# The high part of each weight tile by a casting DMA in the place of a rounding on GpSimd

## The chip, the cores and the metric

The kernel runs on one core of one Trainium2 chip. The metric is the time of one execution in device microseconds (us), as the median of several runs. The engines of a core work side by side, each on its own queue of instructions in a fixed order: TensorE (PE in the profile; PEld is its weight load), VectorE (DVE), ScalarE (ACT), GpSimd (POOL) and SyncE (SP). An instruction waits at the head of its queue until what it needs is there, and all behind it waits with it. DMAs are issued by instructions that stand in such a queue too.

## The reference

The reference is one decoder block for 1024 tokens of 1024 channels: eight heads of forgetting attention and eight of stick-breaking attention, cross-attention to 256 memory tokens, and a gated feed-forward net with a short causal convolution. Cut to its skeleton:

```
h = rmsnorm(x, attn_norm_g)
proj = h @ w_in                       # fq, fk, fv, sq, sk, sv, f_logit
fox_o = forgetting_attention(fq, fk, fv, cumsum(log_sigmoid(f_logit + b_forget)))
sb_o = stick_breaking_attention(sq, sk, sv)
x = x + concat(rmsnorm(fox_o), rmsnorm(sb_o)) @ w_out
x = x + memory_cross_attention(rmsnorm(x), rmsnorm(mem), w_mq, w_mkv, w_mo)
u = causal_dwconv(rmsnorm(x, ffn_norm_g) @ w_up, conv_w, conv_b)
gate, val = split(u)
x = x + (silu(gate) * val) @ w_down
out = rmsnorm(x, final_norm_g)
```

All inputs and the output are float32.

## The kernel before

Matrix products take their operands in the type fp32r, which holds fewer bits than float32. To keep the accuracy, each operand is split into a high part (the value rounded to fp32r) and a low part (the value less its high part), and each product is three matmuls: high by high, high by low, low by high (`mm3`, L100 to L104).

The weights lie in DRAM as pieces of 128 partitions by 1024 columns of float32, 512 KB each, in the order of use (`w[i]`). In the first half of the program a piece is fetched by `getw(i)`, the function that `make_w` returns (L88 to L98). It takes two tiles of 128x1024, `whi` and `wlo`, from a pool with two buffers of each, and works in two halves of 512 columns: SP issues the DMA of the raw half into a tile `wraw` (L94, a pool of three), POOL rounds it into `whi` (L95), DVE subtracts to get `wlo` (L96). `getw` is called 68 times: for the values (`load_v`, two pieces per pair of heads, both in use together), the queries and keys (`load_qk`, one piece each), the keys and values of the memory (L434 on, eight and eight pieces), the projection of the mixed heads (`mixed_out`, four calls of two pieces that are in use together to the end of the call), the queries to the memory (`mem_probs`, two times eight pieces) and a part of the output projection of the memory heads (two times two pieces). With two buffers, the tile of piece n is filled again for piece n+2, once the last matmul on piece n is through. The tiles of raw halves have a pool of their own, so a raw half can be in SBUF while its `whi` is still in use. From the rest of the output projection on, weights are loaded in other ways, and `getw` is not called again.

What else stands on POOL in this half: the multiplication of each stick-breaking row by its running product (L334), the division of each forgetting row by its sum (L320), the power -0.5 of the norms (L86), and the division of the memory's probabilities (L550). What else stands on DVE: the low parts of the attention's rows (L363), the running products (L332), maxima and sums.

The order of each engine's instructions is not that of the source. A scheduler places them, with its own estimates of how long each takes; it interleaves matmuls on weights with those of the attention, so a piece can be filled while PE has other work. That order is fixed when the program is built.

Of the kernel before, what the change touches and what calls it, by code (L numbers as in the profile page):

```python
# [29 lines left out]
# pairs of heads: one of each kind shares the projection of the values  # L30
KINDS = ("s", "f")

# columns of the per-channel parameters
# [11 lines left out]
def hybrid_block(ctx, tc, x, mem, w, wf, pcol, bfg, fing, out):  # L45
# [14 lines left out]
    # ---------------- constants  # L60
# [20 lines left out]
    # ---------------- helpers  # L81
    def rsqrt_mean(dst, ss, n, cnt):
        """dst = (ss / cnt + eps) ** -0.5 for n columns"""
        V.tensor_scalar(out=dst[:, :n], in0=ss[:, :n], scalar1=1.0 / cnt, scalar2=EPS,
                        op0=ALU.mult, op1=ALU.add)
        G.tensor_tensor(dst[:, :n], dst[:, :n], mhalf[:, :n], op=ALU.pow)  # L86

    def make_w(rp, wp):  # L88
        def get(i):
            hi = wp.tile([P, 1024], F32R, tag="whi", name=f"whi{i}")  # L90
            lo = wp.tile([P, 1024], F32R, tag="wlo", name=f"wlo{i}")
            for c in (slice(0, 512), slice(512, 1024)):
                raw = rp.tile([P, 512], F32, tag="wraw", name=f"wraw{i}", bufs=3)
                nc.sync.dma_start(raw, w[i, :, c])  # L94
                G.tensor_scalar(out=hi[:, c], in0=raw, scalar1=1.0, scalar2=0.0, op0=ALU.mult, op1=ALU.add)  # L95
                V.tensor_tensor(lo[:, c], raw, hi[:, c].bitcast(F32), op=ALU.subtract)  # L96
            return hi, lo
        return get  # L98

    def mm3(o, lt, rt, start, stop):  # L100
        """o += l^T r for operands in two exact parts"""
        T.matmul(o, lt[0], rt[0], start=start, stop=False)  # L102
        T.matmul(o, lt[0], rt[1], start=False, stop=False)  # L103
        T.matmul(o, lt[1], rt[0], start=False, stop=stop)  # L104

    def split(hi, lo, ps, scale):
        """hi + lo = ps * scale, exactly"""
        if isinstance(scale, float):
            A.activation(hi, ps, AF.Copy, scale=scale)
        else:  # L110
            A.activation(hi, ps, AF.Identity, scale=scale)
        V.scalar_tensor_tensor(out=lo, in0=ps, scalar=scale, in1=hi.bitcast(F32),
                               op0=ALU.mult, op1=ALU.subtract)

    def norm_half(src_tiles, gcol, hi, lo, pst, wk, n=4, tags=(("T", 2),), xtag="xn", eng=V):
        """rmsnorm of n blocks of tokens, transposed into hi/lo [P, KC, n*P]"""
        ss = small.tile([P, 4], F32, tag="ss", name="ss")
        rs = small.tile([P, 4], F32, tag="rs", name="rs")
        xn = []
        for j in range(n):  # L120
            xs = src_tiles[j]
            t = wk.tile([P, D], F32, tag=xtag, name="xn")
            A.activation(t, xs, AF.Square, accum_out=ss[:, j:j + 1])
            rsqrt_mean(rs[:, j:j + 1], ss[:, j:j + 1], 1, D)
            if eng is V:
                V.tensor_scalar(out=t, in0=xs, scalar1=rs[:, j:j + 1], scalar2=None, op0=ALU.mult)
            else:
                G.tensor_scalar(out=t, in0=xs, scalar1=rs[:, j:j + 1], scalar2=0.0, op0=ALU.mult, op1=ALU.add)
            xn.append(t)
        for kc in range(KC):  # L130
            tg, nb = tags[kc % len(tags)]
            pt = pst.tile([P, 512], F32, tag=tg, name="ptn", bufs=nb)
            for j in range(n):
                T.transpose(pt[:, j * P:(j + 1) * P], xn[j][:, kc * P:(kc + 1) * P], ident)
            split(hi[kc], lo[kc], pt[:, :n * P], col(gcol + kc))

    # ================= token mixing =================
# [3 lines left out]
    # four slots of [P, 4096] for the transposed activations; the last pair's queries, keys and  # L141
    # values leave room for eight more tiles of [P, 1024]
# [20 lines left out]
    def eight(nm, n):  # L163
        """eight tiles of [P, 1024] as two lists of n views"""
        t = [qkp["s"].tile([P, 1024], F32R, tag=g, name=f"{nm}_{g}{i}", bufs=b)
             for g, b, i in (("q", 2, 0), ("q", 2, 1), ("k1", 2, 0), ("k1", 2, 1), ("k2", 1, 0))]
        v5 = vp.tile([P, 2, 1024], F32R, tag="v", name=nm + "_v0")
        v7 = vp.tile([P, 2, 1024], F32R, tag="v", name=nm + "_v1")
        t += [v5[:, 0, :], v5[:, 1, :], v7[:, 0, :]]
        w_ = 4096 // n  # L170
        t = [x_[:, c:c + w_] for x_ in t for c in range(0, 1024, w_)]
        return t[:n], t[n:]
# [47 lines left out]
    # forget gates: -cumsum(log sigmoid(f + b)) as [head, token]  # L220
    def forget():
# [12 lines left out]
        # -log sigmoid(z) = max(-z, 0) + ln(1 + exp(-|z|))  # L234
# [4 lines left out]
    def load_v(pr):  # L239
        """values of a pair of heads of each kind, [token, block, head, hi|lo]"""  # L240
# [21 lines left out]
    def load_qk(kind, pr):  # L262
        """two heads: Q = [hi;lo], K1 = [hi;hi] on the contraction rows; K2 = lo of both"""
# [59 lines left out]
    def sb_row(i, sts, p):  # L323
        """sigmoid(z_s) times the product of 1 - sigmoid(z_j) = sigmoid(-z_j) over j > s"""
# [6 lines left out]
        # running product from the right end; no factor is above 1, so the minimum changes nothing  # L331
# [4 lines left out]
    def attend(kind, h, a, vt, hq, qkt, ost):  # L336
        """one head; the output goes to rows a*64.. of the pair's staging tiles"""
# [51 lines left out]
    for pr in range(4):  # L389
        vt = load_v(pr)  # L390
        for ki, kind in enumerate(KINDS):
# [9 lines left out]
            for g in range(2):  # L401
# [10 lines left out]
                # squares, summed over the pairs  # L412
# [10 lines left out]
    # memory keys and values  # L423
# [28 lines left out]
    # ================= projection of the mixed heads =================  # L452
# [59 lines left out]
    # ================= attention to the memory =================  # L512
# [67 lines left out]
    # the output projection of the memory heads has the form of the feed-forward net's (below): a = the  # L580
    # heads' outputs (halves of the tokens x halves of the channels), b = the weights
# [24 lines left out]
    # in the order b11, b12, b22, b21  # L606
# [4 lines left out]
    # t1 and t3 in the places of b11 and b12  # L611
# [11 lines left out]
    def pairs(t):  # L623
        """[hi | lo] of an operand of [P, 512]"""
        return t[:, :512], t[:, 512:]
# [12 lines left out]
    def mo_product(fa, fb, tags, done, deep=False):  # L638
        """fa(f), fb(f): the operands' values for the channels f; done(j, bank) for each 128 tokens"""
# [47 lines left out]
    # ================= feed-forward net =================  # L687
    # up: products of 2 x 2 blocks (gate | value channels, halves of the contraction, halves of the
    # tokens) in Winograd's form of Strassen's scheme, seven products of blocks in the place of eight:
    #   [c11 c12]   [a11 a12] [b11 b12]     s1 = a21 + a22, s2 = s1 - a11, s3 = a21 - a11, s4 = a12 - s2  # L690
    #   [c21 c22] = [a21 a22] [b21 b22]     t1 = b12 - b11, t2 = b22 - t1, t3 = b12 - b22, t4 = b21 - t2
    #   c11 = a11 b11 + a12 b21             u = a11 b11 + s2 t2, v = u + s3 t3
    #   c12 = u + s1 t1 + s4 b22            c21 = v + a22 t4,    c22 = v + s1 t1
# [42 lines left out]
    # operands of the weights  # L736
# [73 lines left out]
    # second half of the tokens  # L810
# [123 lines left out]
    # down: the same scheme with a = the activations (halves of the tokens x halves of the channels)  # L934
    # and b = the weights (halves of the channels x halves of the outputs); a product runs over all of
    # its channels in four banks, one for 128 tokens of each half
# [10 lines left out]
    # first and second half: a11 | a21 and b11 | b12, later a12 in the place of a11, b21 in that of b11  # L947
# [34 lines left out]
    def op_tile(nm):  # L982
        """[hi | lo] of an operand"""
        tag = ("whi" if nm == "a" else "wlo") if step % 2 == 0 else "xn"
        pool = wp if step % 2 == 0 else wk
        return pairs(pool.tile([P, 1024], F32R, tag=tag, name=f"op{nm}"))

    def dn_product(fa, fb, held=0, done=None):
        """fa(f), fb(f): the operands' values for the channels f; the last held of them are used bank
        by bank, done(j, bank) after each"""  # L990
# [25 lines left out]
    # p1 = a11 b11  # L1016
# [3 lines left out]
    # p7 = (a21 - a11) (b12 - b22)  # L1020
# [5 lines left out]
    # p5 = (a21 + a22) (b12 - b11)  # L1026
# [6 lines left out]
    # p6 = s2 t2  # L1033
# [9 lines left out]
    # p3 = s4 b22  # L1043
# [25 lines left out]
    # p4 = a22 t4: the second half of the tokens is done  # L1069
# [5 lines left out]
    # p2 = a12 b21  # L1075
# [7 lines left out]
def arrange(inputs):  # L1083
    """Lays the inputs out in the order in which the kernel reads them."""
    import numpy as np

    def lhs(m):  # [K, 128] -> [128, K/128, 128]
        return m.reshape(-1, P, m.shape[1]).transpose(1, 0, 2).reshape(P, -1)

    def blocks(m, k, c):  # [K, c] in pieces of k row blocks -> [n, 128, k*c]  # L1090
        return [lhs(m[i * k * P:(i + 1) * k * P]) for i in range(m.shape[0] // (k * P))]
# [60 lines left out]
```

## Time and profile before

| | us |
|---|---|
| median of 3 runs | 1697.02 |
| lowest and highest run | 1696.34 and 1701.86 |
| span of the profiled execution | 1694.0 |

The page gives no other time of the profiled execution than its span; the median of the runs lies 3.0 us above it. The page and the answers of the trace name instructions by line, engine, operation, and out<-in by the names in the program; "x136" counts them. Behind a group's busy time and the mean duration of one stands the idle time of the engine just before them, with what ended it. In a timeline, each row has its start, its length, and in brackets the idle time ahead of it.

### The profile page before, as it was taken

Reading aid. Unit: us, or ns where it says so; the run is one execution under the profiler, and the core shown is the slowest. Engines: PE = TensorE matmul, PEld = TensorE weight load, DVE = VectorE, ACT = ScalarE, POOL = GpSimd, SP = SyncE. Lnnn points to the kernel's source line nnn. Section 1 sums busy time; section 2 is a strip of 40 time slices with the busy share of each in tenths; the row PEclk is TensorE's granted clock in tenths of the full one; section 3 lists DMA queues with packets and bytes.
Section 4 is the critical chain, followed back from the end, with each engine's and each line's share of the span. In section 5 each row is a group of like instructions: output and inputs, shape, how many; then the busy total and the mean of one; then the engine's idle time right before and its main releaser. Section 6 shows DMA issues by size and latency. Waiting matters only on the chain.

```text
span 1694.0 us, 21858 instructions
## 1 busy us (share of the span) xinstructions
PE 1620.6 (96%) x7812; PEld 1283.0 (76%) x7812; DVE 1279.3 (76%) x1889; ACT 720.2 (43%) x1414; POOL 714.0 (42%) x634
## 2 busy tenths in 40 slices
PE   7999999999999999999999888999999999989987
PEld 7676876877787877778887666878888888867766
DVE  6377677658667876455547989998888888898796
ACT  7266456546646433033323354333333333434344
POOL 2143233315324551123139568454455452273761
PEclk9999998999899999999999998999999999999999
DMA  4321110112115554512141111222222224811112
GB/s 172 112 64 38 51 62 26 63 51 62 38 56 196 164 176 144 199 50 78 48 139 66 63 51 50 105 82 75 96 79 88 77 75 183 311 56 56 50 63 100
DMA packets 59917, 157.32 MB, mean 93 GB/s; under 512 B 6680, under 2 KB 6808, under 8 KB 59552
## 3 DMA queue, kind: packets, MB, share of 16 engines
q1 hardware_dynamic: 58224, 151.58, 25.2%
q10 hardware_dynamic: 1584, 4.34, 1.1%
q8 instruction: 62, 1.02, 0.2%
q14 instruction: 47, 0.39, 0.1%
HBM read 118.11 MB, written 33.59 MB: 90 GB/s over the span
## 4 chain that ended last, share of the span: by engine, by line
PE 68%; DVE 13%; issue 7%; POOL 6%; DMA 4%; ACT 1%; POOLq 0%; SPq 0%; DVEq 0%; ACTq 0%
PE up_p L103 6%; PE up_p L104 6%; PE up_p L102 6%; PE st L300 4%; PE pq L104 4%; PE pq L102 4%; PE pq L103 4%; PE pt L358 3%; PE po L365 2%; PE po L364 2%; PE st L299 2%; PE dn L103 2%; PE pv L102 2%; PE dn L104 2%; PE pv L104 2%
## 5 line engine op out<-in xcount | busy, mean ns | idle before, releaser
L95 POOL TENSOR_SCALAR whi<-wraw 128x512 fp32r<-128x512 f32 x136 | 93.3, 698 | 269.7 <-issue 121.4
L96 DVE TENSOR_TENSOR wlo<-wraw,whi 128x512 fp32r<-128x512 f32 x136 | 121.5, 900 | 53.2 <-POOL whi L95 52.8
L363 DVE TENSOR_TENSOR ptl<-pt,pth 128x512 fp32r<-128x512 f32 x192 | 103.2, 550 | 64.0 <-ACT pth L362 56.4
L334 POOL TENSOR_TENSOR p<-p,aw 128x127 f32<-128x127 f32 (+3 forms) x64 | 91.1, 1429 | 140.7 <-DVE aw L332 96.6
L362 ACT ACTIVATE pth<-pt 128x512 fp32r<-128x512 f32 x192 | 91.9, 492 | 130.3 <-PE pt L358 103.1
L103 PE MATMUL dn<-opb,opa 128*128 128x512 f32 x308 | 124.8, 405 | 9.9 <-DVE opb L636 9.9
L104 PE MATMUL dn<-opb,opa 128*128 128x512 f32 x308 | 120.6, 397 | 1.8 <-DVE opa L636 1.7
L102 PE MATMUL dn<-opb,opa 128*128 128x512 f32 x308 | 113.4, 394 | 5.1 <-ACT opb L633 4.4
L332 DVE TENSOR_TENSOR_SCAN aw<-aw 128x128 f32<-128x128 f32 (+3 forms) x64 | 102.3, 1603 | 17.0 <-ACT aw L329 16.5
L320 POOL TENSOR_SCALAR p<-p,rsum 128x128 f32<-128x128 f32 (+3 forms) x64 | 52.8, 827 | 122.5 <-DVE rsum L319 109.0
L358 PE MATMUL pt<-ident,p 128*128 128x128 f32 x576 | 96.5, 282 | 1.9 <-DVE ptl L363 1.9
L785 POOL TENSOR_TENSOR tmp<-wv 128x512 f32<-128x512 f32 x21 | 40.0, 1904 | 131.6 <-DMA wv<-in_w_dram 123.7
L103 PEld LDWEIGHTS dn<-opb,opa 128*128 128x128 f32 x308 | 59.3, 192 | 29.4 <-DVE opb L636 17.3
L358 PEld LDWEIGHTS pt<-ident,p 128*128 128x128 f32 x576 | 70.8, 144 | 12.4 <-DVE ptl L363 2.6
L365 PE MATMUL po<-ptl,v 128*128 128x512 f32 x192 | 73.2, 385 | 1.3 <-DVE ptl L363 1.2
L364 PE MATMUL po<-pth,v 128*128 128x512 f32 x192 | 72.2, 376 | 1.5 <-DVE ost L368 1.5
L102 PEld LDWEIGHTS dn<-opb,opa 128*128 128x128 f32 x308 | 58.2, 190 | 19.0 <-ACT opb L633 5.5
L311 DVE CUSTOM_DVE_ANT_0 p<-st,negc 128x512 f32<-128x512 f32 (+2 forms) x96 | 52.3, 553 | 26.5 <-PE st L302 12.6
L102 PE MATMUL up_p<-b,a 128*128 128x512 f32 x176 | 68.8, 393 | 1.2 <-DVE cg L833 0.7
L104 PEld LDWEIGHTS dn<-opb,opa 128*128 128x128 f32 x308 | 58.8, 192 | 14.6 <-DVE opa L636 3.0
L103 PE MATMUL up_p<-b,a 128*128 128x512 f32 x176 | 68.6, 390 | 0.0
L104 PE MATMUL up_p<-b,a 128*128 128x512 f32 x176 | 68.3, 390 | 0.0
(501 smaller groups left out, 5230.7 us busy)
## 6 DMA issues: line engine op xcount, KB each, us to landing
wraw<-in_w_dram SPq DMA_DIRECT2D x136, 256.0 KB, 2.8
a_d<-yv SPq DMA_DIRECT2D x22, 512.0 KB, 2.6
wv<-in_w_dram SPq DMA_DIRECT2D x21, 512.0 KB, 3.6
wg<-in_w_dram SPq DMA_DIRECT2D x20, 512.0 KB, 3.5
xin<-in_x_dram SPq DMA_DIRECT2D x8, 512.0 KB, 4.5
negc<-negc_d SPq DMA_DIRECT2D x8, 512.0 KB, 4.2
xs<-in_x_dram SPq DMA_DIRECT2D x8, 512.0 KB, 3.7
x_d<-xs SPq DMA_DIRECT2D x8, 512.0 KB, 3.1
```

Source lines behind the costliest of these rows:

```text
L95: G.tensor_scalar(out=hi[:, c], in0=raw, scalar1=1.0, scalar2=0.0, op0=ALU.mult, op1=ALU.add)
L96: V.tensor_tensor(lo[:, c], raw, hi[:, c].bitcast(F32), op=ALU.subtract)
L102: T.matmul(o, lt[0], rt[0], start=start, stop=False)
L103: T.matmul(o, lt[0], rt[1], start=False, stop=False)
L104: T.matmul(o, lt[1], rt[0], start=False, stop=stop)
L332: V.tensor_tensor_scan(out=a[:, ::-1], data0=a[:, ::-1], data1=a[:, ::-1], initial=1.0, op0=ALU.mult, op1=ALU.min)
L334: G.tensor_tensor(p[:, :w_ - 1], p[:, :w_ - 1], a[:, 1:], op=ALU.mult)
L358: T.transpose(pt[:, j * P:(j + 1) * P], rows[j][:, kb * P:(kb + 1) * P], ident)
L362: A.activation(th_[:, c], pt[:, c], AF.Copy)
L363: V.tensor_tensor(tl_[:, c], pt[:, c], th_[:, c].bitcast(F32), op=ALU.subtract)
L364: T.matmul(po[:, c], vt[:, kb, hq, :], th_[:, c], start=kb == 0, stop=False)
L365: T.matmul(po[:, c], vt[:, kb, hq, :], tl_[:, c], start=False, stop=kb == nkb - 1)
```

## The change

The rounding on POOL goes. In its place, ahead of the two raw halves, POOL issues one DMA of the whole piece from DRAM into `whi`; the DMA casts from float32 to fp32r. The raw halves are still loaded on SP, and DVE still subtracts `whi` from them. Besides this, comments and blank lines change, so that line numbers behind `getw` are higher by one; the new DMA is L93, SP's load of a raw half L96 and DVE's subtraction L97.

```
@@ -89,22 +89,23 @@
         def get(i):
             hi = wp.tile([P, 1024], F32R, tag="whi", name=f"whi{i}")
             lo = wp.tile([P, 1024], F32R, tag="wlo", name=f"wlo{i}")
+
+            nc.gpsimd.dma_start(hi, w[i])
             for c in (slice(0, 512), slice(512, 1024)):
                 raw = rp.tile([P, 512], F32, tag="wraw", name=f"wraw{i}", bufs=3)
                 nc.sync.dma_start(raw, w[i, :, c])
-                G.tensor_scalar(out=hi[:, c], in0=raw, scalar1=1.0, scalar2=0.0, op0=ALU.mult, op1=ALU.add)
                 V.tensor_tensor(lo[:, c], raw, hi[:, c].bitcast(F32), op=ALU.subtract)
             return hi, lo
         return get
...
```

The scheduler places the rest anew. Behind the middle of the output projection of the memory heads, the instructions on PE, DVE, ACT, POOL and SP stand in the same order as before. Ahead of it they are interleaved in another way. The start of POOL's queue, before (`whi_155` and `whi_169` are the first two pieces):

```order
masks.py:197 MEMSET ident 128x128
masks.py:199 ISA
masks.py:199 AFFINE_SELECT ident<-ident 128x128
L207 AFFINE_SELECT mask_f<-zb 128x128
L209 AFFINE_SELECT mask_s<-zb 128x128
L86 TENSOR_TENSOR rs<-rs,mhalf 128x1
L95 TENSOR_SCALAR whi_155<-wraw_157 128x512
L86 TENSOR_TENSOR rs<-rs,mhalf 128x1
L95 TENSOR_SCALAR whi_155<-wraw_161 128x512
```

The same place with the change, where the first two pieces are `whi_155` and `whi_168`:

```order
masks.py:197 MEMSET ident 128x128
L93 DMA whi_155<-in_w_dram 128x1024
L93 DMA whi_168<-in_w_dram 128x1024
masks.py:199 ISA
masks.py:199 AFFINE_SELECT ident<-ident 128x128
L208 AFFINE_SELECT mask_f<-zb 128x128
L210 AFFINE_SELECT mask_s<-zb 128x128
L86 TENSOR_TENSOR rs<-rs,mhalf 128x1 x9
```

The two DMAs stand at the very start of the queue now, with nothing to wait for, and the norms' powers follow without a rounding between them.

PE's queue from the last use of the first piece of the third call of `mixed_out` to the first use of its buffer's next piece, before (`whi_7445` and `whi_7455` are the pieces of the third call, `whi_7601` is the first of the fourth, and takes the buffer of `whi_7445`):

```order
L104 MATMUL pm<-whi_7445,mxf_v_6121 128x512
L102 MATMUL pm<-whi_7455,mxf_k_6118 128x512
L103 MATMUL pm<-wlo_7456,mxf_k_6118 128x512
L104 MATMUL pm<-whi_7455,mxf_v_6121 128x512
L102 MATMUL pm<-whi_7455,mxf_k_6119 128x512
L103 MATMUL pm<-wlo_7456,mxf_k_6119 128x512
L104 MATMUL pm<-whi_7455,mxf_v_6122 128x512
L102 MATMUL pm<-whi_7601,mxf_q_6116 128x512 x2
L103 MATMUL pm<-wlo_7602,mxf_q_6116 128x512
```

The same place with the change (`whi_7401`, `whi_7410` and `whi_7555` are the same three pieces):

```order
L105 MATMUL pm<-whi_7401,mxf_v_6097 128x512
L103 MATMUL pm<-whi_7410,mxf_k_6094 128x512
L104 MATMUL pm<-wlo_7411,mxf_k_6094 128x512
L105 MATMUL pm<-whi_7410,mxf_v_6097 128x512
L103 MATMUL pm<-whi_7410,mxf_k_6095 128x512
L104 MATMUL pm<-wlo_7411,mxf_k_6095 128x512
L105 MATMUL pm<-whi_7410,mxf_v_6098 128x512
L103 MATMUL pm<-whi_7555,mxf_q_6092 128x512 x3
L104 MATMUL pm<-wlo_7556,mxf_q_6092 128x512
```

Here six matmuls stand between the release of the buffer and its next use, in both programs; what moved is that one matmul more on the high part follows ahead of the first on the low part.

PE's queue at the release of the first piece of the first call of `mixed_out`, with the change (`whi_7093` and `whi_7102` are its pieces, `whi_7235` is the first of the second call; `po` belongs to the attention):

```order
L105 MATMUL pm<-whi_7093,mxsl 128x512
L103 MATMUL pm<-whi_7102,mxsh 128x512
L104 MATMUL pm<-wlo_7103,mxsh 128x512
L105 MATMUL pm<-whi_7102,mxsl 128x512
L103 MATMUL pm<-whi_7102,mxsh 128x512
L104 MATMUL pm<-wlo_7103,mxsh 128x512
L105 MATMUL pm<-whi_7102,mxsl 128x512
L365 MATMUL po<-pth,v_5091 128x256
L366 MATMUL po<-ptl,v_5091 128x256
L365 MATMUL po<-pth,v_5091 128x128
L366 MATMUL po<-ptl,v_5091 128x128
L103 MATMUL pm<-whi_7235,mxsh 128x512 x2
```

Before, eight transposes of the attention's rows (L358) stood between these four matmuls on `po` and the next piece as well; with the change they stand elsewhere.

More of the change, by code (lines that the diff above doesn't have):

```diff
@@ L91, in get @@
             lo = wp.tile([P, 1024], F32R, tag="wlo", name=f"wlo{i}")
+            nc.gpsimd.dma_start(hi, w[i])
             for c in (slice(0, 512), slice(512, 1024)):
@@ L94, in get @@
                 nc.sync.dma_start(raw, w[i, :, c])
-                G.tensor_scalar(out=hi[:, c], in0=raw, scalar1=1.0, scalar2=0.0, op0=ALU.mult, op1=ALU.add)
                 V.tensor_tensor(lo[:, c], raw, hi[:, c].bitcast(F32), op=ALU.subtract)
```

## The prediction

> **What bounds the kernel now.** I read the page's parts 1 and 4 first, then stretches of the span side by side, then the groups of the lines that the change touches.
>
> ```profile
> span 1694.0 us, 21858 instructions
> PE 1620.6 (96%) x7812; PEld 1283.0 (76%) x7812; DVE 1279.3 (76%) x1889; ACT 720.2 (43%) x1414; POOL 714.0 (42%) x634
> PE 68%; DVE 13%; issue 7%; POOL 6%; DMA 4%; ACT 1%; POOLq 0%; SPq 0%; DVEq 0%; ACTq 0%
> 0.00:45.00 45.00, 35.52 (x264) 33.03 (x265) 30.58 (x81) 31.14 (x76) 11.97 (x25) 1.00 0.45 162
> 45.00:545.00 500.00, 494.99 (x2569) 374.22 (x2567) 335.76 (x642) 265.62 (x588) 158.04 (x160) 0.98 0.20 66
> 545.00:629.00 84.00, 83.74 (x491) 66.74 (x491) 70.75 (x142) 40.34 (x90) 47.90 (x54) 1.00 0.52 167
> 629.00:746.00 117.00, 112.03 (x532) 89.61 (x530) 63.85 (x117) 25.45 (x48) 20.67 (x29) 1.00 0.45 154
> 746.00:906.00 160.00, 157.27 (x832) 132.67 (x833) 87.34 (x130) 54.20 (x133) 56.68 (x83) 1.00 0.25 85
> 906.00:1694.00 788.00, 737.05 (x3131) 586.77 (x3130) 691.01 (x779) 303.41 (x481) 418.71 (x289) 0.97 0.25 91
> L95 POOL TENSOR_SCALAR whi<-wraw 128x512 fp32r<-128x512 f32 x136 | 93.3, 698 | 269.7 <-issue 121.4
> L96 DVE TENSOR_TENSOR wlo<-wraw,whi 128x512 fp32r<-128x512 f32 x136 | 121.5, 900 | 53.2 <-POOL whi L95 52.8
> ```
>
> A window's row gives its length, then the busy time of PE, PEld, DVE, ACT and POOL, the granted clock, the DMA engines' share and GB/s. The chain of what ended last is 68% PE. All 136 roundings lie before 907 us, and there PE is the bound: from 45 to 906 us it is idle for 5.0 + 0.3 + 5.0 + 2.7 = 13 us in 861. So POOL's 93.3 us run beside matmuls; removing them can return a part of those 13 us and no more. The other idle time lies in the first 45 us (9.5) and behind 906 us (51), where the order of the instructions stays as it was. What can cost is a weight that comes later than PE wants it.
>
> **What a refill costs before.** Where two pieces are used together to the end of a pass, PE comes to the next piece a few matmuls after its buffer is free.
>
> ```profile
> 718.71 0.39 PE L102 MATMUL pm<-whi,mxf_k 128*128 128x512 f32 x1
> ...
> 719.02 1.21 POOL L95 TENSOR_SCALAR whi<-wraw 128x512 fp32r<-128x512 f32 x2 [13.37 <-issue]
> ...
> 719.67 2.11 DVE L96 TENSOR_TENSOR wlo<-wraw,whi 128x512 fp32r<-128x512 f32 x2 [1.38 <-POOL whi L95]
> 719.84 0.39 PE L104 MATMUL pm<-whi,mxf_v 128*128 128x512 f32 x1
> 720.07 0.61 PE L102 MATMUL pm<-whi,mxf_q 128*128 128x512 f32 x2
> ...
> 720.82 0.50 PE L103 MATMUL pm<-wlo,mxf_q 128*128 128x512 f32 x1
> ```
>
> This timeline is the seam between the third and the fourth projection pass. The raw half waits in SBUF, POOL rounds it while PE does its last six matmuls, and PE goes on at 720.07 without a gap. Five steps from 718.71 to 719.84 make a 512-column matmul 0.226 us. With the change the buffer must be free before POOL can issue the DMA, the whole 512 KB must land, and then DVE subtracts: the data that waited in SBUF before now starts from DRAM.
>
> **The late places.** In the new order I counted PE's work between the last use of a buffer and the first use of its next piece, for all 66 refills. At five it is under 2.5 us. Three more, the second pieces at these places, have 3.1 to 4.1, on top of which comes the first one's wait. Of the rest one has 4.6, the others 5 and more.
>
> ```profile
> 24.82 0.28 PE L102 MATMUL pv<-whi,h_0h 128*128 128x256 f32 x1
> 25.17 0.28 PE L102 MATMUL pv<-whi,h_0h 128*128 128x256 f32 x1
> 702.79 0.94 PE L376 MATMUL pss<-ones,sqaccf 128*128 128x1 f32 x8
> 742.51 1.04 PE L134 MATMUL ptn<-ident,xn 128*128 128x128 f32 x8
> ```
>
> Three steps from 24.82 to 25.17 make a 256-column matmul 0.117 us. The five are: first query piece after the first values, twelve such matmuls, 1.40 us; second projection pass, six long matmuls and four short ones, 1.36 + 0.47 = 1.83; third pass, six and the eight of `pss`, 1.36 + 0.94 = 2.30; fourth pass, six, 1.36; first query piece of the memory, six and eight transposes, 1.36 + 1.04 = 2.40. The sum is 9.3 us. With a refill of L us from the free buffer to the landed high part, PE stands for **5 L - 9.3 us** there. The low part's first use follows by 0.5 to 1.3 us in the order, about the time of its subtraction, so it adds nearly nothing.
>
> **The size of L.** No POOL-issued DMA is in this trace, and none that casts. The nearest rows are SP's loads and POOL's own instructions.
>
> ```profile
> wv<-in_w_dram SPq DMA_DIRECT2D x21, 512.0 KB, 3.6
> wg<-in_w_dram SPq DMA_DIRECT2D x20, 512.0 KB, 3.5
> xin<-in_x_dram SPq DMA_DIRECT2D x8, 512.0 KB, 4.5
> dnq<-in_w_dram SPq DMA_DIRECT2D x2, 512.0 KB, 10.7
> 33.52 1.13 POOL L128 TENSOR_SCALAR xn<-mrow,rs 128x1024 f32<-128x1024 f32 x1
> 34.61 0.55 POOL L86 TENSOR_TENSOR rs<-rs,mhalf 128x1 f32<-128x1 f32 x1
> ```
>
> The same bytes, a weight piece of 512 KB, land 3.5 us after issue where the queue is free, 4.5 where it is crowded and 10.7 behind a burst. That is the range of L: 3.5 (POOL's issue and the cast for nothing) to 10.7. I take 3.5, plus 1.1 for POOL's work of making the DMA (its pass over 128x1024 takes 1.13, its smallest operation 0.55), plus half of the crowding, 0.5, since SP refills raw halves at the same moments: **L = 5.1, and 5 x 5.1 - 9.3 = +16.2 us**. The row nearest to this is `wg`; the issue and the cast are what it lacks.
>
> The Trainium skill (DMA: Bandwidth & Descriptors, Anatomy of one DMA — SWDGE (gpsimd) path) puts a GpSimd-issued DMA at about 2.0 us fixed plus its bytes over 436e3 per us. For 524,288 bytes that is an estimate of 3.2 us, and the five places would cost 5 x 3.2 - 9.3 = 6.7 us. SP's 3.5 here is above it; no row here shows a POOL issue.
>
> **The start.** Two whole pieces, 1 MB, now go out at the very start, ahead of most of the tokens.
>
> ```profile
> 0.72 4.47 DMA xin<-in_x_dram
> 0.72 0.87 SPq L183 DMA_DIRECT2D xin<-in_x_dram  x2
> 1.64 0.93 SPq L94 DMA_DIRECT2D wraw<-in_w_dram  x2
> 2.61 2.93 SPq L183 DMA_DIRECT2D xin<-in_x_dram  x2
> 5.58 0.43 SPq L94 DMA_DIRECT2D wraw<-in_w_dram  x1
> ```
>
> The chain of the span begins with the first token load, 4.47 us. SP issues 4 x 512 + 3 x 256 KB, 2.75 MB, in 6 us; if they are through by about 9 us that is some 0.3 MB per us, and 1 MB more in the same engines is up to 3.3 us. The first tokens are ahead of it and later ones behind: bounds 0 and 3.3, I take **+2**.
>
> **What comes back.** PE's waits for weights go into the new, longer ones, and the roundings leave POOL's chain where that chain counts, at the output projection of the memory heads.
>
> ```profile
> 695.79 0.50 PE L103 MATMUL pm<-wlo,mxf_q 128*128 128x512 f32 x1 [0.58 <-DVE wlo L96]
> 743.93 0.71 PE L102 MATMUL pqm<-h_0h,whi 128*128 128x512 f32 x2 [0.39 <-POOL whi L95]
> 899.76 2.20 POOL whi L95 x3
> 906.60 0.61 POOL whi L95
> ```
>
> The two waits are 0.97 us: **-1.0**. The four roundings on the chain are 2.8 us; two issues take their place, at 0.55 to 1.13 each by the POOL rows above, so -0.5 to -1.7; I take **-1.1**. Elsewhere POOL's roundings are hidden by PE's matmuls, and I cost their going at nothing, with the 5.0 us of PE idle time from 45 to 545 us as the most they could return. The extra traffic, 68 x 0.5 = 34 MB, adds 5% of the page's 16 engines' time in all and is costed only at the start. A POOL instruction behind a waiting DMA waits as it did behind a waiting rounding: the rows' products and divisions, and through them PE's transposes. DVE is the new queue at risk: a subtraction that waits for its DMA holds the running products and low parts of the attention behind it. Where PE's cover is 5 us or more I cost that at nothing; if the cover is gone, it is the third rival.
>
> **Sum.** 16.2 + 2 - 1.0 - 1.1 = +16.1 us on a span of 1694.0, that is 1710.1; the runs' median is 3.0 above the span, so **1713 us**.
>
> **Rivals.** *No change.* L is 3.5, the start costs nothing, and POOL's relief returns the 5.0 us of idle time in the attention: 8.2 - 1.0 - 1.7 - 5.0 = +0.5, 1697.5 us. For it: the start's token loads were issued first. Against: a POOL issue would have to be as quick as SP's. The formula of the Trainium skill cited above (DMA: Bandwidth & Descriptors, Anatomy of one DMA — SWDGE (gpsimd) path) would lead to about this time. *Faster.* POOL free of 93.3 us lets rows of the attention reach PE sooner, and half of the 13 us of idle time comes back; that needs L near 2.5 (5 x 2.5 - 9.3 = 3.2): 3.2 - 1.0 - 1.7 - 6.5 = -6, 1691 us. It decides at L below about 3 us, under every 512 KB load above. *Late everywhere.* The cast slows the transfer, L is about 8. Then the five places cost 30.7 us, and some two dozen refills with 4.6 to 7.5 us of cover are late too, by about 1.5 us each before neighbours share a wait, say 25 us together: +55, 1752 us. For it: `dnq` at 10.7, 167 GB/s already in the memory's keys and values, where sixteen pieces follow at 5 us each. *Not what it says.* If POOL is held as long by an issue as by two roundings (1.4 us), or if the cast left the high part unrounded, the five places and the time would be as forecast.
>
> **Chances.** Forecast (1702 to 1735) 0.53; no change 0.18; faster 0.11; late everywhere 0.18. A difference under 0.3%, 5 us, can hardly be told from none: below 1692 counts as faster (0.11), up to 1702 as same (0.18), above as slower (0.71). With L from 3.5 to 10.7 and all else at its ends, the five places alone run from 1698 to 1744; I extend the range to 1696 and 1750, which leaves out the faster case and about half of the late one.
>
> **What would show it.** Right: PE idle ahead of `pm<-whi` at three seams of the projection, 3 us or so each, ended by a DMA; one such wait near 46 us at the first `pq`; landing of `whi` near 5 us in the list of DMA issues; PE without new waits elsewhere. Wrong: landings under 3 us or over 7; DVE idle before L97 for much more than the 53 us of before; a first matmul that is no later. The forecast fails most easily by L, which no row here measures.

## The result: 1739.4 us, 2.4% slower than before

| | us, median (range) | ratio to before, 95% interval |
|---|---|---|
| before | 1697.72 (1696.34 to 1701.86) | |
| changed | 1739.4 (1734.28 to 1742.62) | 1.0241 (1.0224 to 1.0258) |

The forecast was 1713, that is +16 us; it is +41.7. The time lies inside the range given, and the sign is the one forecast. The size is off by a factor of two and a half. The profiled execution of the changed kernel, 1742.62 us, is the longest of its four runs, so the two profiled spans below lie 46.9 us apart where the medians lie 41.7 apart.

### The profile after

The page of the changed kernel: span and busy times, the chain of what ended last, the two groups of the change (the subtraction and the new DMA), and from the list of DMA issues the median time to landing.

```profile
span 1740.9 us, 21771 instructions
PE 1634.7 (94%) x7812; PEld 1291.3 (74%) x7812; DVE 1256.3 (72%) x1889; ACT 721.1 (41%) x1414; POOL 652.6 (37%) x566
PE 59%; DVE 14%; DMA 11%; issue 8%; POOL 5%; ACT 2%; SPq 0%; POOLq 0%; DVEq 0%; ACTq 0%
...
L97 DVE TENSOR_TENSOR wlo<-wraw,whi 128x512 fp32r<-128x512 f32 x136 | 102.8, 784 | 113.1 <-DMA whi<-in_w_dram 91.4
L93 POOL DMA_DIRECT2D whi<-in_w_dram x68 | 38.8, 570 | 342.4 <-PE pq L105 93.4
...
whi<-in_w_dram POOLq DMA_DIRECT2D x68, 512.0 KB, 4.8
```

PE executes the same 7812 matmuls. The span is 46.9 us longer than before, and these lines split it without a remainder: PE is **busy** 1634.7 - 1620.6 = 14.1 us longer, and **idle** 106.2 - 73.4 = 32.8 us longer (span less busy, in each). The idle part is what the forecast was about. The busy part, the same matmuls taking longer, was in none of its terms.

For the idle part, the view of waits of PE in the changed kernel, the rows of 1 us and more that name a weight (total, times, longest):

```profile
PE pm L103 <- DMA whi<-in_w_dram: 10.3, 3, 3.6
PE pq L103 <- DMA whi<-in_w_dram: 7.2, 1, 7.2
PE pmo L103 <- DMA whi<-in_w_dram: 3.9, 1, 3.9
PE pm L104 <- DVE wlo L97: 3.2, 1, 3.2
PE pk L103 <- DMA whi<-in_w_dram: 2.9, 2, 2.4
PE pv L103 <- DMA whi<-in_w_dram: 2.5, 3, 1.0
PE pqm L103 <- DMA whi<-in_w_dram: 2.1, 1, 2.1
PE pmv L103 <- DMA whi<-in_w_dram: 1.3, 1, 1.3
```

They make 33.4 us, and two smaller rows on `wlo` bring them to 34.0. Before, the rows on weights make 2.2 us (`pmo` 1.2, `pm` 0.6, `pqm` 0.4). So 31.8 of the 32.8 us are waits for weights. The five places of the forecast are the rows `pq` (first query piece), `pm` L103 (three seams of the projection) and `pqm`: 19.6 us. The other five rows, 13.8 us, are waits that the forecast put at nothing.

For the busy part, the windows view of the changed kernel at seven stretches, one at each of these waits of 2 us and more but the one for `wlo`; the column behind POOL's is the granted clock:

```profile
50.60:57.50 6.90, 3.60 (x9) 2.86 (x10) 1.99 (x3) 0.00 (x0) 0.00 (x0) 0.51 0.79 243
569.50:576.30 6.80, 5.49 (x22) 4.77 (x22) 2.78 (x5) 1.06 (x3) 0.76 (x1) 0.50 0.71 169
695.80:699.20 3.40, 3.06 (x7) 2.44 (x8) 1.96 (x3) 0.63 (x1) 0.00 (x0) 0.51 0.90 297
723.10:729.90 6.80, 4.08 (x10) 3.24 (x11) 3.78 (x9) 0.00 (x0) 2.05 (x2) 0.50 1.06 396
757.20:760.60 3.40, 3.40 (x10) 2.59 (x9) 1.62 (x4) 0.00 (x0) 0.00 (x0) 0.50 0.69 192
784.50:787.90 3.40, 3.40 (x12) 2.82 (x11) 2.20 (x4) 1.33 (x2) 0.00 (x0) 0.50 0.65 199
944.90:951.80 6.90, 5.44 (x15) 4.40 (x16) 4.41 (x2) 0.38 (x1) 4.58 (x5) 0.51 0.38 106
sum 37.60, PE 28.47 PEld 23.11 DVE 18.73 ACT 3.40 POOL 7.38; mean PE 4.07 PEld 3.30 DVE 2.68 ACT 0.49 POOL 1.05
```

Wherever PE waits for 2 us or more for a high part, it is granted half its clock from some point within the wait, or up to 1 us behind it, for 3.4 or 6.8 us. PE is busy for 28.5 us of these stretches, at half speed, so the same work would have taken 14.2 us less. These waits are paid twice, once in idle time and once more in slow matmuls. The wait of 3.2 us for `wlo` brought no half speed, and `fill2` below has a wait of 2.6 us at `mo` (a later stage) without it, where the changed kernel has it at a wait of 2.6 us; so a wait of this length doesn't always bring it.

That the 14.2 us are so near to the 14.1 of the busy part is chance, since the kernel before has stretches at half clock too: three in the attention, where no wait is longer than 1 us, and the others behind 946 us. The sums over all stretches at half clock, before and changed:

```profile
sum 64.13, PE 51.92 PEld 38.97 DVE 48.63 ACT 22.48 POOL 39.19; mean PE 4.72 PEld 3.54 DVE 4.42 ACT 2.04 POOL 3.56
sum 89.36, PE 69.43 PEld 55.55 DVE 56.65 ACT 22.28 POOL 33.42; mean PE 4.34 PEld 3.47 DVE 3.54 ACT 1.39 POOL 2.09
```

PE works 69.4 us at half speed in place of 51.9, so 8.8 us more are lost. That is the part of the 14.1 us that the clock explains; the other 5.3 us were not taken apart. What brings the half speed in the attention, in both kernels, is not shown.

The first refill shows a wait that is paid twice. The timeline of the changed kernel (start, length, engine and line; in brackets the idle time before it and what ended that):

```profile
45.09 0.33 SPq L205 DMA_DIRECT2D mT_d<-mT  x1
45.63 0.62 POOL L93 DMA_DIRECT2D whi<-in_w_dram  x1 [8.71 <-PE pv L105]
...
53.90 0.76 PE L103 MATMUL pq<-h_0h,whi 128*128 128x512 f32 x1 [7.17 <-DMA whi<-in_w_dram]
...
54.46 0.63 PE L104 MATMUL pq<-h_0l,whi 128*128 128x512 f32 x1
...
54.89 0.63 PE L103 MATMUL pq<-h_1h,whi 128*128 128x512 f32 x1
...
57.45 0.41 PE L103 MATMUL pq<-h_0h,whi 128*128 128x512 f32 x1
...
57.69 0.39 PE L104 MATMUL pq<-h_0l,whi 128*128 128x512 f32 x1
```

POOL issues the DMA at once when PE frees the buffer, at 45.63, but PE can only go on at 53.90: 8.3 us for the refill, where the forecast had 5.1. Half a microsecond ahead of it SP sent off the 2 MB store of the memory's tokens. Then the matmuls follow each other at 0.43 us until 57.45, and at 0.24 from there.

### The profile page after: what moved, and what is told of

It is laid out like the page before. It is cut to its first block, busy times and chain, and to the rows that moved or that the text cites. A ratio compares the mean times of both kernels' runs of the same rounds, so it can differ in the third digit from the quotient of the medians.

```text
span 1740.9 us, 21771 instructions
## 1 busy us (share of the span) xinstructions
PE 1634.7 (94%) x7812; PEld 1291.3 (74%) x7812; DVE 1256.3 (72%) x1889; ACT 721.1 (41%) x1414; POOL 652.6 (37%) x566
## 4 chain that ended last, share of the span: by engine, by line
PE 59%; DVE 14%; DMA 11%; issue 8%; POOL 5%; ACT 2%; SPq 0%; POOLq 0%; DVEq 0%; ACTq 0%
PE up_p L103 6%; PE up_p L104 6%; PE up_p L105 6%; DMA whi<-in_w_dram 5%; PE pq L103 3%; PE pq L105 3%; PE pq L104 3%; PE st L301 3%; PE pt L359 3%; PE dn L104 2%; PE po L366 2%; PE dn L105 2%; PE dn L103 2%; PE pqm L103 2%; PE pqm L105 2%
## 5 line engine op out<-in xcount | busy, mean ns | idle before, releaser
L97 DVE TENSOR_TENSOR wlo<-wraw,whi 128x512 fp32r<-128x512 f32 x136 | 102.8, 784 | 113.1 <-DMA whi<-in_w_dram 91.4
L93 POOL DMA_DIRECT2D whi<-in_w_dram x68 | 38.8, 570 | 342.4 <-PE pq L105 93.4
L104 PE MATMUL dn<-opb,opa 128*128 128x512 f32 x308 | 124.8, 405 | 10.0 <-DVE opb L637 9.9
L103 PE MATMUL dn<-opb,opa 128*128 128x512 f32 x308 | 113.4, 393 | 5.1 <-ACT opb L634 4.4
L333 DVE TENSOR_TENSOR_SCAN aw<-aw 128x128 f32<-128x128 f32 (+3 forms) x64 | 93.5, 1467 | 21.0 <-ACT aw L330 20.4
L104 PEld LDWEIGHTS dn<-opb,opa 128*128 128x128 f32 x308 | 59.3, 192 | 29.4 <-DVE opb L637 17.3
L103 PEld LDWEIGHTS dn<-opb,opa 128*128 128x128 f32 x308 | 58.2, 190 | 19.1 <-ACT opb L634 5.5
L103 PE MATMUL up_p<-b,a 128*128 128x512 f32 x176 | 68.9, 393 | 1.1 <-DVE cg L834 0.7
L104 PE MATMUL up_p<-b,a 128*128 128x512 f32 x176 | 68.6, 390 | 0.0
L330 ACT ACTIVATE aw<-st 128x512 f32<-128x512 f32 (+2 forms) x96 | 47.4, 496 | 42.7 <-PE st L303 19.0
```

The costliest lines, as they stand in the source:

```text
L333: V.tensor_tensor_scan(out=a[:, ::-1], data0=a[:, ::-1], data1=a[:, ::-1], initial=1.0, op0=ALU.mult, op1=ALU.min)
```

## The experiments

Two theories and four rivals. **Latency**: a refill that begins only at the free buffer is late wherever its cover is short. **Clock**: what such a wait costs on top is the half speed behind it. Rivals: **traffic** (each piece is read from DRAM twice), **VectorE's order** (subtractions that wait hold up the attention), **GpSimd's order** or a price of each POOL-issued DMA, and **bursts** of other DMAs at the refill. A fifth rival has no run: the scheduler's new order by itself, without the DMA. The waits that don't name a weight differ by 1.0 us in all, so the new order can have little of the idle part, but it may have some of the 5.3 us of busy time that are open. The times are shown as microseconds above the runs of before on the same chip, with the ratio's interval; the changed kernel is +41.7.

| kernel | us | above before | ratio, 95% interval |
|---|---|---|---|
| deep2 | 1741.7 | +44.9 | 1.0240 to 1.0297 |
| noraw | 1735.0 | +38.2 | 1.0199 to 1.0247 |
| lofree | 1744.2 | +47.4 | 1.0258 to 1.0314 |
| dupd | 1777.8 | +81.1 | 1.0452 to 1.0505 |
| deep4 | 1728.0 | +30.0 | 1.0150 to 1.0194 |
| early2 | 1729.9 | +31.8 | 1.0171 to 1.0214 |
| fill2 | 1719.6 | +21.5 | 1.0109 to 1.0172 |
| halves | 1724.2 | +26.1 | 1.0139 to 1.0178 |
| nostore | 1730.8 | +34.4 | 1.0182 to 1.0218 |
| bfill | 1710.8 | +14.4 | 1.0066 to 1.0098 |
| deephalf | 1714.4 | +18.0 | 1.0085 to 1.0129 |
| covered | 1695.4 | -2.2 | 0.9980 to 1.0001 |

### Traffic, VectorE's order, and the same bytes alone

```
 noraw:  - raw = ...; nc.sync.dma_start(raw, w[i, :, c])
         - V.tensor_tensor(lo[:, c], raw, hi[:, c].bitcast(F32), op=ALU.subtract)
         + V.tensor_tensor(lo[:, c], hi[:, c].bitcast(F32), hi[:, c].bitcast(F32), op=ALU.subtract)
 lofree: - V.tensor_tensor(lo[:, c], raw, hi[:, c].bitcast(F32), op=ALU.subtract)
         + V.tensor_tensor(lo[:, c], raw, raw, op=ALU.subtract)
```

> The changed kernel without the plain loads; the low parts are computed from the high part alone (zero), so the traffic is that of the kernel before, all of it issued by GpSimd. Traffic theory: the landings fall from 4.8 us to about 3.7 and most of the loss goes, 1700 to 1712 us. Latency theory: the landings may fall a little, but each refill still starts at the free buffer, 1722 to 1735 us; the landing in the stretch 560 to 780 us decides how much of it.

> The changed kernel with the low part computed as raw minus raw (zero), so that VectorE's instruction no longer waits for the casting DMA; DMAs, buffers and instruction counts are the same. VectorE theory (its 113 us of waiting ahead of the subtractions, 60 more than before, hold the attention's low parts and running products): 10 us or more return, 1720 to 1730 us. Latency theory: PE waits for the high part itself, so at most the 3.2 us at pm L104 return, 1734 to 1741 us.

Without the second reading the landing falls from 4.8 to 4.2 us and the time by 3.5 us, at the upper end of the latency theory's bounds. But PE starts 3.5 us later in `noraw`, at 11.18 in place of 7.72, which the edit brought with it. Without that, some 7 us would have come back, by an estimate from these numbers; traffic is a small part either way.

```profile
whi<-in_w_dram POOLq DMA_DIRECT2D x68, 512.0 KB, 4.2
```

This is the row of `noraw` in the list of issues.

`lofree` lies outside both ranges, at +47.4. It has a wait of PE that the changed kernel lacks:

```profile
PE pom L104 <- DVE ptm L113: 8.3, 1, 8.3
```

The same row has 0.2 us in the changed kernel. DVE's row holds three subtractions ahead of `ptm` that take 7.7 us together, where one takes 0.7 in the median; why is not shown. Less this wait and half of the 5.3 us that PE works at half speed behind it, `lofree` would be at about +36.5, some 5 us under the changed kernel (an estimate). The VectorE theory asked for 10 or more, so it can be no large part, but the run doesn't put it at nothing.

`dupd` was to add the traffic alone to the kernel before:

```
+ dup = dram.tile([P, 1024], F32, name=f"dup{i}")
+ nc.gpsimd.dma_start(dup, w[i])
```

> The kernel before, with a GpSimd-issued copy of each piece (512 KB, DRAM to DRAM, no cast) next to it that nothing waits for: the extra traffic and GpSimd's issues alone, more of it since it is also written to DRAM. Traffic theory: most of the loss, 1722 to 1745 us. Latency theory: little, 1697 to 1708 us.

It missed its purpose. Since nothing gates these copies, all 68 were issued between 1.3 and 120 us and landed after 13.8 us in the median, on top of the start; PE waited 41 us for the first tokens, and 27 and 16 us for roundings that POOL's row held behind the copies. It says nothing of traffic spread over the stages, and is no evidence for that theory.

### More buffers

`deep2` gives every second piece from the memory's keys on another buffer, from the attention (`aw`, then `q`), and for the last ones from the next pool (`xn`):

```
+ far = i % 2 and (24 <= i < 40 and (sw, "aw") or 40 <= i < 44 and (qkp["f"], "q")
+                  or 44 <= i < 48 and (wk, "xn"))
+ hi = (far[0] if far else wp).tile([P, 1024], F32R, tag=far[1] if far else "whi", ...)
```

> The changed kernel with four high-part buffers in place of two from the memory's keys to the end of the two projections (pieces 24 to 47); attention and all behind 790 us as in the changed kernel. Latency theory (a refill starts only when its buffer is free, and then takes 5.4 us): the 22 us of delay that grow between 560 and 780 us mostly go, 1718 to 1724 us, PE's waits for whi in the projection under 3 us in all. Traffic theory (the second reading of each piece slows every landing there): the same bytes in the same stretch, 1732 us or more. POOL's order theory (DMAs in POOL's row hold the attention's products and divisions): no change either, 1735 to 1742.

It failed as a test. The waits of `pk` and `pmv` for weights are gone, but two new ones came with the edit: the piece for which PE waits longest was issued only at 729.27, behind two powers of the norm (L86) in POOL's row that had waited 5.26 us for DVE, and its buffer lies where the attention's had been (which of the two held it is not shown); and the token rows of the projection (`xs`) lost their buffers. In its view of waits:

```profile
PE pm L103 <- DMA whi<-in_w_dram: 7.9, 1, 7.9
...
PE pm L103 <- DVE xs L474: 3.1, 1, 3.1
```

`deep4` does the same with other places, meant to be free in time (`hv` is a buffer of the values):

```
+ if i in (46, 47): hi = hv[0][:, i % 2, :]
+ else:
+     far = 24 <= i < 44 and i % 4 > 1
+     hi = (sw if far else wp).tile([P, 1024], F32R, tag="aw" if far else "whi", ...)
- xs = sw.tile([P, D], F32, tag="aw", name="xs")
+ xs = sw.tile([P, D], F32, tag="negc", name="xs")
```

> The changed kernel with buffers for the high parts of later pieces where they fit without a new wait: pieces 26, 27, 30, 31, 34, 35, 38, 39, 42 and 43 in buffers of the attention that are free by then (the token rows of the projection move to another), 46 and 47 in one of the values. In the changed kernel TensorE's waits for weights from 560 to 780 us are 18 us, and granted half speed there is 17 us long, a loss of 8. Latency theory (the refill starts too late): at least 12 us of the waits go, with them part of the slow clock, 1718 to 1727 us. Rival (the waits only move, since low parts, raw halves or the attention's rows are late next): 1734 to 1742 us.

11.7 us less than the changed kernel, 1 us outside what latency expects, and 6 from the rival. Its view of waits has four rows on weights, and one on the token rows that the changed kernel has with 0.4 us alone:

```profile
PE pq L104 <- DMA whi<-in_w_dram: 7.2, 1, 7.2
...
PE pm L104 <- DVE xs L473: 3.8, 2, 3.5
...
PE pmo L104 <- DMA whi<-in_w_dram: 2.8, 1, 2.8
...
PE pm L105 <- DVE wlo L100: 1.7, 2, 1.1
...
PE pv L104 <- DMA whi<-in_w_dram: 0.9, 2, 0.6
```

The waits for weights fall from 34.0 to 12.6 us, but the one at the second projection pass, 3.5 us in the changed kernel, is there again at 3.5 us, for `xs` now. The rival is right at that one place.

`early2` takes the first refill alone; pieces 2 and 3 load at the start:

```
+ early = i in (2, 3)
+ hi = (qkp["f"] if early else wp).tile([P, 1024], F32R, tag="q" if early else "whi", ...)
```

> The changed kernel with the first two query and key pieces (2 and 3) in two buffers that stand empty, so that they load at the start. Latency theory: the 7.2 us wait at the first pq and the slow matmuls behind it (4 more us lost by 58 us) go, less up to 3 us for 1 MB more in the start's burst; 1730 to 1735 us. Rival (the start's burst takes it back, or the attention behind absorbs what it wins): 1737 to 1742 us.

9.9 us less, for a wait of 7.2: as latency and clock together expect (the time is 0.1 us below their range).

### The burst at the first refill

`nostore` leaves out the store, SP's L205, and loads other data where it is read back:

```
- nc.sync.dma_start(mT_d..., mT_...)
...
- nc.sync.dma_start(mT_..., mT_d...)
+ for j, kc in enumerate((0, 1, 2, 4)):
+     nc.sync.dma_start(mT_[:, 2 * j:2 * j + 2, :]..., mix_d[0][kc]...)
```

> The changed kernel without the 2 MB store of the memory's normalised tokens ahead of the first pq; where they are read back, four pieces of the mixed heads are read in their place, so the memory's keys and values are of other data. The rest of the order is the same. Burst theory (the first refill lands after 8.1 us since that store is on its way): the landing falls to 3.7 to 5 us, the wait of 7.2 us at the first pq to 3 to 4, 1733 to 1737 us. Rival (the first refill is slow by itself): landing and time as in the changed kernel, 1738 to 1742 us.

Its timeline at the same place:

```profile
44.02 0.62 POOL L93 DMA_DIRECT2D whi<-in_w_dram  x1 [8.72 <-PE pv L105]
...
48.04 0.77 PE L103 MATMUL pq<-h_0h,whi 128*128 128x512 f32 x1 [2.93 <-DMA whi<-in_w_dram]
```

From issue to PE's next matmul it is 4.0 us, against 8.3 with the store. The burst is shown to be what made the first refill long; the kernel is 7.3 us faster for it, more than the wait itself lost (4.2).

### Fillers: the clock by itself

`fill2` keeps the late refills and gives PE something to do while it would wait for them, 44 matmuls ahead of the first `pq` and 20 transposes ahead of each of the passes 2, 3 and 4 of the projection:

```
+ idle = ps.tile([P, 512], F32, tag="O", name="idle", bufs=1)
+ for _ in range(44):
+     T.matmul(idle[:, :256], hT[0][0][0][:, :P], v0[0][:, TB - 1]..., start=True, stop=True)
...
+ if last:
+     for _ in range(20):
+         T.transpose(idle[:, :P], last[0], ident)
```

> The changed kernel with matmuls and transposes of no use, whose results nothing reads, in TensorE's order ahead of the first pq (44 of 256 columns) and of the second, third and fourth projection pass (20 of 128 each); they wait for the last evacuation before the seam and run while TensorE would wait for the weight. Clock theory (TensorE is granted half speed after a wait, and that loss comes on top of the wait): no half speed from 50 to 58 us, the first pf some 2 us earlier, half speed ahead of the mo stage 10 to 20 us shorter, 1730 to 1736 us. Rival (half speed comes by a schedule of its own, whatever TensorE does): as the changed kernel, or slower by up to 5 us, 1738 to 1745 us.

104 useless instructions on the busiest engine make the kernel 20 us faster. The windows of the changed kernel, then of `fill2`, over the first refill and over 440 to 950 us; the clock stands behind the five engines:

```profile
44.00:62.00 18.00, 10.83 (x52) 9.03 (x51) 4.57 (x10) 1.32 (x5) 1.16 (x2) 0.81 0.69 233
440.00:950.00 510.00, 479.90 (x2458) 384.10 (x2458) 288.06 (x559) 182.56 (x412) 123.13 (x156) 0.97 0.50 159
```

```profile
44.00:62.00 18.00, 16.40 (x100) 14.32 (x99) 3.90 (x9) 1.33 (x4) 1.16 (x2) 1.00 0.67 234
440.00:950.00 510.00, 493.30 (x2596) 397.07 (x2595) 302.07 (x562) 187.24 (x416) 138.78 (x165) 1.00 0.49 162
```

No half speed is left there. The waits without fillers have none either; they are also shorter than before: `pmo` 1.3 us in place of 3.9, `pk` 1.7 in place of 2.9. Over the whole trace PE works 32.8 us at half speed in place of 69.4, so 18.3 us less are lost. The two profiled spans lie 25.0 us apart; the rest is idle time, which falls by 19.3 us (from 106.2 to 86.9), more than the some 13 that the fillers themselves take. Half speed doesn't follow from waits of this kind alone, though: it is still there three times in the attention. The control has the same fillers in the kernel before, which has no such waits at these places:

> The kernel before, with the same useless matmuls and transposes as in the run with fillers; there TensorE has no long waits at these places. If the fillers win in the changed kernel because they fill its waits, here they only add their own time, 44 of 0.117 and 60 of 0.13 us or 13 us at most: 1702 to 1711 us. Rival (any more work on TensorE raises the granted clock): 1697 us or less.

There they cost 14.4 us, about their own length. So they win in the changed kernel by filling its waits, and the rival that any work raises the clock is out.

### The size of the DMA, and both remedies

```
 halves: - nc.gpsimd.dma_start(hi, w[i])
         + nc.gpsimd.dma_start(hi[:, :512], w[i, :, :512])
         + nc.gpsimd.dma_start(hi[:, 512:], w[i, :, 512:])
```

> The changed kernel with the casting DMA cut into two of 256 KB, one for each half of the columns; the first matmuls need the first half alone. If the size of the transfer makes the refill long, the first half lands a good 1 us sooner and a dozen waits are shorter by that, 1725 to 1733 us. If the fixed part and the issue do (0.57 us each, twice as many), 1738 to 1750 us.

```profile
whi<-in_w_dram POOLq DMA_DIRECT2D x136, 256.0 KB, 3.7
```

The halves land after 3.7 us instead of 4.8, and 15.6 us come back, 1 us more than expected. But the waits are not shorter everywhere: at the three seams of the projection they make 10.7 us, 10.3 in the changed kernel. What is won lies elsewhere, above all at the first `pq`, 1.7 us in place of 7.2. The timeline there shows that part of it is luck of the order, since SP's 2 MB store now goes out behind the DMAs:

```profile
45.14 0.62 POOL L92 DMA_DIRECT2D whi<-in_w_dram  x1 [9.76 <-PE pv L105]
45.76 0.54 POOL L93 DMA_DIRECT2D whi<-in_w_dram  x1
...
47.40 0.33 SPq L205 DMA_DIRECT2D mT_d<-mT  x1
...
48.18 0.47 PE L103 MATMUL pq<-h_0h,whi 128*128 128x512 f32 x1 [1.71 <-DMA whi<-in_w_dram]
```

What twice as many DMAs in GpSimd's queue cost can't be told apart in this run.

> The changed kernel with both of what helped: the buffers for later pieces from the memory's keys on, and the casting DMA in two halves. If refill latency and the slow clock behind it are the loss, the gains of 11 and 15 us add up but for the projection's waits, which both shorten: 1710 to 1717 us. Rival (twice as many DMAs in GpSimd's row take it back): 1720 us or more. Below the kernel before, 1698, in neither case.

`deephalf` is `deep4` with `halves`: of the two gains, 27.3 us, 23.7 are there, and 1714.4 is in the range. It is the best of the kernels that cast every piece without fillers, and still behind the kernel before. Its waits for weights are down to 5.7 us; what else keeps it 18 us behind was not taken apart.

### Where the cover is long

`covered` casts only 24 of the 68 loads, those of the second to fourth pair's queries and keys and of the memory's queries but for the first two pieces, and rounds the others as before:

```
+ cast = i in (8, 9, 10, 11, 14, 15, 16, 17, 20, 21, 22, 23) or 50 <= i < 56
+ if cast: nc.gpsimd.dma_start(hi, w[i])
...
+     if not cast: G.tensor_scalar(out=hi[:, c], in0=raw, ...)
```

> The cast only where TensorE has much other work between the last use of a buffer and the first of its next piece: the query and key pieces of the second to fourth pair of heads, and the memory's query pieces but for the first two; 24 of 68 loads. The others are rounded on GpSimd as in the kernel before. Latency theory (a refill costs only where its cover is short): 1695 to 1702 us, waits for whi of under 2 us in all. Rival (each casting DMA costs something, by its traffic or in GpSimd's row): 24 / 68 of the 42 us, 1708 to 1714 us.

No row of its waits names a DMA of `whi`, and the ratio is 0.9991 (0.9980 to 1.0001). With 24 casting DMAs and their 12 MB of second reading the time can't be told from that of before: the rival's 24 / 68 of the loss is far outside the interval, and where the cover is long the DMA has no price of its own that could be seen.

## Why the prediction was right in sign and wrong in size

- **What bounds the kernel, and that a late refill is the way it loses**: right. `deep4`, `early2` and `covered` show it from three sides.
- **The five late places, 5 L - 9.3 with L = 5.1, +16.2 us**: nearly right. They are the places named, and take 19.6 us. The landing is counted from the start of the issue, so its median gives L = 4.8; the 5.4 of some expectations counts the issue's 0.57 us twice. Four of the five waits lie within 0.9 us of 5.1 less their cover. The fifth, the first `pq`, is 3.5 us longer: the refill took 8.3 us, by a store that the forecast had not looked for at that moment (`nostore`). The Trainium skill's formula (DMA: Bandwidth & Descriptors, Anatomy of one DMA — SWDGE (gpsimd) path) came to 3.2 us; the fastest of the 68 landed after 3.7.
- **"Where PE's cover is 5 us or more I cost that at nothing", and the low part that "adds nearly nothing"**: the first step that failed; 13.8 us of waits, 10.6 for high parts (`pmo`, `pk`, `pv`, `pmv`) and 3.2 for one low part. Three of them can be followed in the timeline of the changed kernel:

```profile
560.84 0.59 POOL L93 DMA_DIRECT2D whi<-in_w_dram  x1
...
570.82 0.58 PE L103 MATMUL pk<-mT,whi 128*128 128x256 f32 x1 [2.42 <-DMA whi<-in_w_dram]
...
731.16 1.37 SPq L96 DMA_DIRECT2D wraw<-in_w_dram  x3
...
737.24 0.69 DVE L97 TENSOR_TENSOR wlo<-wraw,whi 128x512 fp32r<-128x512 f32 x1 [7.72 <-DMA wraw<-in_w_dram]
...
737.99 0.50 PE L104 MATMUL pm<-wlo,mxf_k 128*128 128x512 f32 x1 [3.22 <-DVE wlo L97]
...
938.83 3.32 POOL L615 TENSOR_TENSOR mow<-mow,mow 128x512 f32<-128x512 f32 x2 [4.07 <-DVE mow L614]
...
942.09 0.61 POOL L93 DMA_DIRECT2D whi<-in_w_dram  x1
...
946.36 1.19 PE L103 MATMUL pmo<-whi,om0h 128*128 128x512 f32 x2 [3.94 <-DMA whi<-in_w_dram]
```

At `pk` the refill took 10.0 us from issue to use, more than its cover; from 545 to 629 us the core moves 229 GB/s, 167 before. At `pm` L104 a raw half was late: its buffer is now held until the high part has landed, and its load stood in SP's row among stores and token rows; which of the two made it late was not tried. At `pmo` the DMA stood in POOL's row behind two subtractions that had waited 4.07 us for DVE. The forecast had asked what stands behind a waiting DMA, not what it stands behind.
- **The clock**: the term that was missing. PE's busy time grew by 14.1 us, of which 8.8 are half speed, net of what the kernel before loses by it; the seven waits alone cost 14.2. The forecast read the granted clock in the windows (0.97 to 1.00) and let it stand as a constant of the kernel. `fill2` and `bfill` show that at these places it follows from the waits. The Trainium skill states such a rule (TensorE: Matmul & The Clock Gate, HAM oscillation — how this bites in real kernels): no idle gaps of TensorE above some 3.4 us, or the next matmuls run at half clock. This trace agrees for its long waits, 3.5 to 7.2 us, and goes beyond the rule: `pk` and `pqm` were granted half speed at waits of 2.4 and 2.1 us. Half of the stretches of 3.4 and 6.8 us is 1.7 and 3.4 us, the most that one wait can have lost; 14.2 us at seven waits is 2.0 in the mean, a term that the forecast lacked.
- **The start, +2 us**: wrong in sign, and small. The first `pv` comes 1.1 us earlier, at 10.27 in place of 11.39.
- **What comes back, -1.0 and -1.1**: the old waits for weights are gone, 0.6 and 0.4 us and the 1.2 that PE had waited for a rounding at the memory heads' output projection (`pmo`). But 3.9 us for the DMA stand in its place there.
- **"Late everywhere"**: the time is nearer to this rival, in part for its reason: refills with cover were late too. That the cast itself slows a transfer is not shown, since no run has the same DMA without it; L was 4.8 and not 8. DVE's idle time ahead of the subtractions doubled, from 53 to 113 us, as its mark said; by `lofree` this costs some 5 us at most.

Put together: 34.0 us of waits for weights, less 2.2 for the old ones, and 14.1 us of busy time are 45.9 of the 46.9 us between the two spans. Of the busy time 8.8 us are the clock, and the cause of 5.3 stays open.

## What to carry to other kernels

Before a prefetched copy is replaced by a load into the working buffer, list for each buffer how much work the consumer has between its release and its next use, and compare it with the slowest landing of that stage, not with the median; look at what stands ahead of the DMA in its engine's row, and which bursts leave just then. Where the cover is long the change is free here (`covered`); where it is short, more buffers or a smaller first piece take back a part, 11.7 and 15.6 of 41.7 us and 23.7 with both (`deep4`, `halves`, `deephalf`). A wait of the matmul engine can cost more than its length: count the slow matmuls behind it.

## What the runs showed of the hardware that was not expected

- Half the clock for 3.4 or 6.8 us at the seven waits of 2.1 to 7.2 us for a high part, from within the wait or up to a microsecond behind it; in all 14 us lost, on top of 26 us of waiting at these places. Other waits of 2.6 and 3.2 us had none.
- 104 matmuls and transposes of no use made the changed kernel 20 us faster, and the kernel before 14 us slower.
- One 2 MB store, sent off 0.5 us earlier, made a load of 512 KB take 8.3 us in place of 4.0 until it was used.
